# Another order for the steps of the S5 mixer in a two-layer hybrid encoder trunk

## The chip, the cores and the metric

The kernel runs on one core of a Trainium2 chip. The metric is the device time of one execution in microseconds (us). Five engines work side by side, each through its own queue of instructions and in the order of that queue: TensorE (PE, matmuls and transposes), VectorE (DVE), ScalarE (ACT), GpSimd (POOL) and SyncE (SP, here only an issuer of DMAs). ScalarE issues DMAs too, from the same queue that holds its arithmetic.

## The reference

The sequence has 1024 rows of 1024 channels. Layer 0 mixes the rows with a diagonal complex state-space layer (S5), layer 1 with gated linear attention; each is followed by a squared-ReLU MLP. The change touches the S5 mixer alone:

```python
def s5_mixer(u, a_re, a_im, log_dt, b_re, b_im, c_re, c_im, d_skip, w_glu):
    # 64 groups of 16 channels, each with a 64-dim complex diagonal state
    ...
    _, _, xr, xi = lax.associative_scan(combine, (la_re, la_im, bu_re, bu_im), axis=1)
    y = (jnp.einsum('blgp,ghp->blgh', xr, c_re.astype(f32))
         - jnp.einsum('blgp,ghp->blgh', xi, c_im.astype(f32))
         + d_skip.astype(f32).reshape(S5_GROUPS, S5_GROUP) * uf)
    z = jax.nn.gelu(y.reshape(bsz, seq, D_MODEL)).astype(u.dtype)
    val, gate = jnp.split(z @ w_glu, 2, axis=-1)
    return val * jax.nn.sigmoid(gate)
```

## The kernel before

The 1024 rows are cut into 128 chunks of 8. Within a chunk the mixer is a small Toeplitz matrix applied to the inputs; between chunks a state is carried by a scan over the 128 chunks. The channels go in 8 blocks (0 to 7) of 128 channels, and each block passes through the same kinds of step. Each step is a Python generator, and each of its pieces emits a few instructions; a piece ends at a `yield`. In what follows `s5.3` is the third piece of step `s` of block 5.

- `g` (4 groups only, for two blocks each): the adaLN shift and scale of the mixer's input. g.1 64 matmuls, g.2 and g.6 ACT copies, g.3 and g.5 PE, g.4 small DVE operations.
- `u`: u.1 scales the block's inputs on ACT (8 instructions), u.2 transposes them on PE, u.3 copies them out on ACT (8 instructions).
- `l`: the input matrices. l.1 and l.2 are two DVE products each, l.3 is 32 PE transposes into both banks of the PSUM tag `tp`, l.4 two ACT copies that free these banks.
- `p`: the rotation's sines. p.1 and p.2 DVE, p.3 ACT (Sin, Abs, Sin).
- `e`: the output matrices. e.1 and e.2 two DVE products each, e.3 and e.4 one DVE subtraction each.
- `k`: the Toeplitz block. k.1 PE matmuls into both `tp` banks, k.2 two ACT copies out of them, k.3 a short DVE addition, k.4 two DMAs from ScalarE's queue that write it to a scratch in HBM (`kd<-Ks`), k.5 one DMA from ScalarE's queue that reads it back in overlapping rows (`Tb<-kd`, 512 KB). k.5 waits in ScalarE's queue until what k.4 wrote has landed.
- `s`: the states. s.1 ACT, s.2 PE, s.3 four DVE products, s.4 two DVE additions, s.5 two DVE scans, s.6 four DVE products that give X.
- `o`: the output. o.1 PE matmuls with the Toeplitz block `Tb`, o.2 64 PE matmuls with X, o.3 two ACT Gelus.

Gelu and Sin lie in different activation tables, so ScalarE loads a table (ACT_TABLE_LOAD) wherever o.3 and p.3 take turns.

The order of all these pieces is written out by hand, in the string `S5ORD` (line 739); a loop steps the generators in that order, and a manual schedule keeps each of PE, DVE, ACT and POOL in the order of the string. SP is not in it: its loads start as buffers come free. After s7.6, VectorE splits the weights of the GLU (`wl`), and after z7 (o7.3) the last of them; the fourth weight load waits for a staging buffer. The tile pool `wa`, which holds the split weights, lies where the mixer's small tiles lay (`sp`, with `Ks` among them), so ScalarE's first splits wait for k7.4's write. Then the GLU runs, a long row of matmuls, and after it MLP 0, layer 1 and MLP 1.

The buffers around the change: `tp` 2 PSUM banks, `mm` 6, `tmp` 8, E 4, LBT 3, U 3, Tb 3, `stg` 3, and X, R8 and Ks two each.

Of the kernel before, what the change touches and what calls it, by code (L numbers as in the profile page):

```python
# [43 lines left out]
def trunk_kernel(ctx, tc, x, c, w_ada, b_ada, norm_mix, norm_mlp, s5_a_re, s5_a_im, s5_log_dt, s5_b_re, s5_b_im,  # L44
# [68 lines left out]
    def row(src, tag="row", bufs=3, pool="ww"):  # L113
        t = pools[pool].tile([P, 1024], F32, tag=tag, name="row", bufs=bufs)
        nc.sync.dma_start(out=t, in_=src.to_broadcast([P, 1024]))
        return t
# [195 lines left out]
    def small(shape, dt=F32):  # L312
        n_s[0] += 1
        return sp.tile(shape, dt, name=f"s{n_s[0]}")
# [47 lines left out]
    s1 = small(sh1)  # L362
# [23 lines left out]
    s2 = small(sh1)  # L386
# [349 lines left out]
            wg += [(h[:, 512 * k:512 * k + 512], l[:, 512 * k:512 * k + 512]) for k in range(2)]  # L736
        return wg

    S5ORD = "[ s0 s1 S7 S6 I0 S2 S3 e0 I0 S5 H1:v S0 S4 S1 e0 T0 H0:v T0 g0 l0 u0:am p0:v e0 l0 g0 g0 u0 e0 g0 u1:am p0 g0 e1 g1 g0 p0 p1:v e1 l0 g1 u0 p1 e1 e2 p1 e1 l1 l0 g2 e2 l1 g1 s0 g2 g1 e2 g1 s0 g2 u1 g1 u2:am g3 g2 u1 s0 k0 e2 s0 k0 g3 g2 g3 g2 k0 g3 k0 s2 s0 l1 p2:v e3 k0 l1 l2 g3 p2 s1 g3 l2 p2 k1 s1 u2 k1 o0 u2 k1 s1 l2 k1 u3:am s1 o0 e3 l2 s1 k1 s3 k2 e3 o0 l3 s2 k2 e3 k2 k3 l3 k2 o1 s2 k3 l3 p3:v k2 s2 p3 o1 l3 e4 p3 s2 u3 e4 o1 k3 u3 o2 e4 s2 k3 u4:am s3 e4 l4 o2 s4 s3 k3 l4 k4 o2 u4 p4:v s3 k4 u4 l4 p4 e5 p4 s3 l4 u5:am e5 o3 k4 e5 k4 s4 s5 s3 u5 e5 u6:am o3 l5 s4 k4 u5 k5 l5 o3 p5:v k5 s4 l5 p5 e6 p5 s4 l5 e6 o4 s6 k5 e6 k5 s5 s4 u6 e6 u7:am o4 l6 s5 k5 u6 k6 l6 o4 p6:v k6 s5 l6 p6 e7 p6 s5 l6 e7 o5 s7 k6 e7 k6 s6 s5 u7 e7 o5 k6 l7 u7 s6 k7 o5 l7 k7 p7:v l7 s6 p7 s6 p7 l7 k7 o6 s6 k7 s7 o6 s7 k7 s7 o6 s7 o7 s7 o7 o7 ]"

    kinds = {"u": feed, "l": tab_lb, "e": tab_e, "k": tab_k, "p": rotation, "s": states, "o": output, "g": group, "I": inputs}
    gen = {}
# [1 line left out]
    last = {}  # L744
    for n, w in enumerate(S5ORD.split()):
        if w[1:] != "7":
            continue
        last[w[0]] = n
    for n, w in enumerate(S5ORD.split()):
        if w == "[":  # L750
# [154 lines left out]
    for j in range(4):  # L905
# [29 lines left out]
        if j == 2:  # L935
            g2 = row(modr[0][4])
# [515 lines left out]
    g2 = row(modr[1][4])  # L1452
# [83 lines left out]
```

## Time and profile before

| what | value |
| --- | --- |
| time, median of 3 runs | 2200.97 us (2200.49 to 2201.13) |
| the profiled execution: its own time | 2202.5 us |
| the profiled execution: span | 2200.8 us |
| PE / DVE / ACT / POOL busy, share of the span | 96% / 66% / 32% / 18% |
| TensorE's granted clock, mean | 0.986 |
| the mixer (up to z7) | the first 187.0 us of the span |

Views are of one profiled execution and count from the start of its span. A chain of waits names, step by step, what the end waited for. In a timeline an instruction that found its engine idle has that idle time and its releaser in brackets. ACTq and SPq are the queues' DMA issues.

### The profile page before, as it was taken

The numbers are of one execution on the slowest core, as the hardware profiler recorded it, in microseconds if no ns is written. First come the engines' busy times: TensorE is split into PE (matmuls) and PEld (weight loads), VectorE is DVE, ScalarE is ACT, GpSimd is POOL, SyncE is SP. The second block draws the span as 40 slices with busy tenths as digits, with TensorE's granted clock in tenths as the row PEclk, the third lists the DMA queues.
The fourth block names the chain that finished last, engine by engine and source line by source line (L and its number), as shares of the span: only waits on it lengthen the run. The fifth ranks groups of instructions, "written<-read, shape, count | busy, mean of one in ns | idle before, by whom it ended". The sixth has DMA issues, their size and how long they took to land.

```text
span 2200.8 us, 26747 instructions
## 1 busy us (share of the span) xinstructions
PE 2117.0 (96%) x10857; PEld 1730.6 (79%) x10857; DVE 1448.7 (66%) x2004; ACT 693.9 (32%) x1163; POOL 397.1 (18%) x294
## 2 busy tenths in 40 slices
PE   5988999899999999999899999999999999999998
PEld 4876777778888888888687877787788888888886
DVE  8885767966656656656832266638866665665666
ACT  6673113422222222222521443314322222222223
POOL 0000001222222222222600000001122222222223
PEclk9989999999999999999899999999999999999999
DMA  8224771111112111111353103520111111111112
GB/s 250 58 71 138 233 245 51 49 48 57 48 48 58 48 48 58 49 48 58 129 172 99 49 30 112 170 89 29 48 48 48 58 48 48 58 48 48 58 48 105
DMA packets 107656, 176.58 MB, mean 80 GB/s; under 512 B 10463, under 2 KB 76103, under 8 KB 107469
## 3 DMA queue, kind: packets, MB, share of 16 engines
q1 hardware_dynamic: 97164, 168.71, 24.3%
q10 hardware_dynamic: 10368, 6.16, 1.3%
q8 instruction: 85, 1.39, 0.3%
q14 instruction: 39, 0.31, 0.0%
HBM read 164.45 MB, written 10.40 MB: 79 GB/s over the span
## 4 chain that ended last, share of the span: by engine, by line
PE 86%; DVE 6%; DMA 4%; ACT 2%; issue 1%; POOL 1%; ACTq 0%; SPq 0%; POOLq 0%; DVEq 0%
PE mm L216 27%; PE mm L215 27%; PE mm L217 27%; DVE tmp L56 1%; DMA Tb<-kd 1%; DMA stg<-in_w_ada_dram 1%; PE mm L1362 1%; PE tp L210 1%; DMA kd<-Ks 1%; PE tp L609 1%; PE mm L1342 1%; DVE nk L59 1%; DVE adacc L59 0%; DMA stg<-in_gla_w_out_dram 0%; DVE hT L56 0%
## 5 line engine op out<-in xcount | busy, mean ns | idle before, releaser
L56 DVE TENSOR_TENSOR big<-mm,big 128x512 f32<-128x512 f32 x528 | 343.0, 683 | 91.4 <-PE mm L217 85.5
L216 PE MATMUL mm<-w,a 128*128 128x512 f32 x1024 | 387.8, 392 | 0.9 <-DVE w L56 0.9
L217 PE MATMUL mm<-w,a 128*128 128x512 f32 x1024 | 385.4, 390 | 0.0
L215 PE MATMUL mm<-w,a 128*128 128x512 f32 x1024 | 364.8, 390 | 4.3 <-ACT w L66 4.1
L216 PE MATMUL mm<-l,rg 128*128 128x512 f32 x904 | 355.2, 393 | 5.0 <-DVE l L56 5.0
L217 PE MATMUL mm<-h,rg 128*128 128x512 f32 x904 | 354.1, 392 | 0.5 <-DVE rg L56 0.5
L215 PE MATMUL mm<-h,rg 128*128 128x512 f32 x904 | 350.2, 393 | 2.4 <-ACT h L66 1.8
L56 DVE TENSOR_TENSOR wk<-mm,wk 128x512 f32<-128x512 f32 (+1 forms) x100 | 68.8, 688 | 379.2 <-PE mm L217 320.7
L56 POOL TENSOR_TENSOR wk<-wk 128x512 f32<-128x512 f32 (+1 forms) x122 | 160.3, 1324 | 745.6 <-DMA mod<-wk 317.0
L215 PE MATMUL mm<-wh,hT 128*128 128x512 f32 (+1 forms) x768 | 290.4, 380 | 1.7 <-ACT hT L66 1.1
L217 PE MATMUL mm<-wh,hT 128*128 128x512 f32 (+1 forms) x768 | 289.7, 378 | 0.0
L216 PE MATMUL mm<-wl,hT 128*128 128x512 f32 (+1 forms) x768 | 288.9, 377 | 0.1
L56 POOL TENSOR_TENSOR wk<-wk,row 128x1024 f32<-128x1024 f32 x64 | 163.2, 2551 | 608.4 <-DMA wk<-in_w_ff_dram 399.4
L216 PEld LDWEIGHTS mm<-w,a 128*128 128x128 f32 x1024 | 192.7, 188 | 47.5 <-DVE w L56 8.3
L215 PEld LDWEIGHTS mm<-w,a 128*128 128x128 f32 x1024 | 191.2, 188 | 46.5 <-ACT w L66 5.5
L217 PEld LDWEIGHTS mm<-w,a 128*128 128x128 f32 x1024 | 192.8, 188 | 39.4
L66 ACT ACTIVATE wk<-mm 128x512 f32<-128x512 f32 x140 | 83.5, 598 | 423.5 <-PE mm L217 416.4
L216 PEld LDWEIGHTS mm<-l,rg 128*128 128x128 f32 x904 | 169.9, 188 | 43.4 <-DVE l L56 5.9
L215 PEld LDWEIGHTS mm<-h,rg 128*128 128x128 f32 x904 | 169.8, 188 | 41.4 <-ACT h L66 2.3
L217 PEld LDWEIGHTS mm<-h,rg 128*128 128x128 f32 x904 | 170.0, 188 | 39.0 <-DVE rg L56 0.8
L66 ACT ACTIVATE rg<-wk 128x1024 fp32r<-128x1024 f32 (+1 forms) x126 | 114.2, 951 | 271.7 <-POOL wk L56 270.2
L215 PEld LDWEIGHTS mm<-wh,hT 128*128 128x128 f32 x768 | 144.4, 188 | 39.3 <-issue 3.9
(244 smaller groups left out, 2628.4 us busy)
## 6 DMA issues: line engine op xcount, KB each, us to landing
wk<-in_w_ff_dram SPq DMA_DIRECT2D x128, 512.0 KB
stg<-in_w_ada_dram SPq DMA_DIRECT2D x80, 512.0 KB
stg<-in_gla_w_in_dram SPq DMA_DIRECT2D x17, 512.0 KB
stg<-in_s_w_glu_dram SPq DMA_DIRECT2D x32, 256.0 KB
row<-mod SPq DMA_DIRECT2D x10, 512.0 KB
wada<-in_w_ada_dram SPq DMA_DIRECT2D x9, 512.0 KB
big<-in_x_dram SPq DMA_DIRECT2D x8, 512.0 KB
Tb<-kd ACTq DMA_DIRECT2D x8, 512.0 KB
```

What stands on the lines that cost most here:

```text
L56: (e or V).tensor_tensor(out=out, in0=a, in1=b, op=op)
L59: V.scalar_tensor_tensor(out=out, in0=a, scalar=s, in1=b, op0=op0, op1=op1)
L66: S.activation(out=out, in_=a, func=f, **kw)
L210: ins = T.transpose(pt[:, P * k:P * k + P], h[:, P * (4 * q + k):P * (4 * q + k + 1)], ident)
L215: T.matmul(pst, ah, bh, start=first, stop=False, **kw)
L216: T.matmul(pst, ah, bl, start=False, stop=False, **kw)
L217: return T.matmul(pst, al, bh, start=False, stop=last, **kw)
L609: T.matmul(pts[i][:, P * q:P * q + P], t[i][k][:, P * q:P * q + P], (nident if i < k else ident), start=q == 0 and k == 0, stop=q == 3 and ...
L1342: T.matmul(kvp[c2][hp2][:, 256 * (h % 2):256 * (h % 2) + 256], kz[t % 2][cr, P * h:P * h + P], vo[cr, t, 256 * h:256 * h + 256], start=Tru ...
L1362: T.matmul(op[h // 2][64 * c2:64 * c2 + 64, 256 * (h % 2):256 * (h % 2) + 256], qT[:, h, n0:n0 + 64], Sc[c2][:, h, :], start=True, stop=True)
```

## The change

One string is replaced by another. Both hold the same 264 entries, each kind and block with the same number of pieces and on the same engines; the first 24 (up to e0.3) are the same. No instruction, size or buffer differs.

```diff
-    S5ORD = "[ s0 s1 S7 S6 I0 S2 S3 e0 I0 S5 H1:v S0 S4 S1 e0 T0 H0:v T0 g0 l0 u0:am p0:v e0 l0 g0 g0 u0 e0 g0 u1:am p0 g0 e1 g1 g0 p0 p1:v e1 l0 g1 u0 p1 e1 e2 p1 e1 l1 l0 g2 e2 l1 g1 s0 g2 g1 e2 g1 s0 g2 u1 g1 u2:am g3 g2 u1 s0 k0 e2 s0 k0 g3 g2 g3 g2 k0 g3 k0 s2 s0 l1 p2:v e3 k0 l1 l2 g3 p2 s1 g3 l2 p2 k1 s1 u2 k1 o0 u2 k1 s1 l2 k1 u3:am s1 o0 e3 l2 s1 k1 s3 k2 e3 o0 l3 s2 k2 e3 k2 k3 l3 k2 o1 s2 k3 l3 p3:v k2 s2 p3 o1 l3 e4 p3 s2 u3 e4 o1 k3 u3 o2 e4 s2 k3 u4:am s3 e4 l4 o2 s4 s3 k3 l4 k4 o2 u4 p4:v s3 k4 u4 l4 p4 e5 p4 s3 l4 u5:am e5 o3 k4 e5 k4 s4 s5 s3 u5 e5 u6:am o3 l5 s4 k4 u5 k5 l5 o3 p5:v k5 s4 l5 p5 e6 p5 s4 l5 e6 o4 s6 k5 e6 k5 s5 s4 u6 e6 u7:am o4 l6 s5 k5 u6 k6 l6 o4 p6:v k6 s5 l6 p6 e7 p6 s5 l6 e7 o5 s7 k6 e7 k6 s6 s5 u7 e7 o5 k6 l7 u7 s6 k7 o5 l7 k7 p7:v l7 s6 p7 s6 p7 l7 k7 o6 s6 k7 s7 o6 s7 k7 s7 o6 s7 o7 s7 o7 o7 ]"
+    S5ORD = "[ s0 s1 S7 S6 I0 S2 S3 e0 I0 S5 H1:v S0 S4 S1 e0 T0 H0:v T0 g0 l0 u0:am p0:v e0 e1 g0 g0 e0 u0 g0 u1:am e1 g0 l0 g1 g0 e1 u0 p0 k0 e1 e2 k0 p1:v g1 l0 p0 k0 e2 p1 e2 k0 p1 g2 l1 e2 l0 l1 g2 g1 e3 g2 s0 g1 g2 g1 g3 s0 g1 k0 g2 u1 g2 g3 e3 k1 u2:am e3 s0 k1 u1 l1 k1 s0 k1 p2:v s2 o0 s0 l1 g3 s1 g3 l2 g3 o0 s1 g3 k1 l2 k2 o0 e3 u2 p2 s1 k2 p2 l2 k2 s1 e4 k2 u2 o1 s1 l2 l3 o1 u3:am e4 l3 k2 s3 p3:v k3 e4 o1 s2 p3 e4 u3 e5 k3 p3 l3 s2 u3 k3 s2 l4 k3 l3 s2 u4:am k4 s3 e5 k4 s2 o2 s4 u4 l4 k3 o2 u5:am s3 u4 e5 l4 p4:v k4 e5 o2 p4 s3 k4 l4 e6 p4 k5 s3 s4 l5 o3 k5 s5 s3 u5 k4 u6:am e6 o3 l5 u5 s4 l5 o3 e6 p5:v k5 e6 k5 p5 l5 s4 p5 k6 e7 s5 s4 u6 k6 u7:am o4 l6 s4 k5 s6 u6 e7 o4 l6 s5 l6 o4 e7 p6:v k6 p6 k6 l6 e7 s5 p6 k7 s6 l7 s5 u7 k7 u7 o5 l7 s5 l7 k6 s7 s6 o5 l7 p7:v k7 p7 k7 s6 p7 s7 s6 o5 s7 o6 k7 s6 s7 o6 s7 s7 o6 o7 o7 o7 ]"
```

In words: the Toeplitz blocks' pieces come earlier in most of the blocks, with more work of other steps between k.4, k.5 and o.1, and the output matrices e of the early blocks come earlier. VectorE's work in the string between k.4 and k.5, and between k.5 and o.1, is for blocks 0 to 7 in microseconds (pieces taken at e.1 1.2, e.2 1.2, e.3 0.6, e.4 0.6, l.1 1.2, l.2 1.2, p.1 0.6, p.2 1.06, s.3 2.4, s.4 1.2, s.5 2.25, s.6 2.4, k.3 0.1, g.4 0.5):

| | 0 | 1 | 2 | 3 | 4 | 5 | 6 | 7 |
| --- | --- | --- | --- | --- | --- | --- | --- | --- |
| k.4 to k.5, before | 4.2 | 5.9 | 3.0 | 4.2 | 6.6 | 6.6 | 3.0 | 2.4 |
| k.4 to k.5, after | 7.6 | 7.1 | 6.0 | 7.1 | 7.1 | 9.3 | 8.9 | 5.9 |
| k.5 to o.1, before | 5.9 | 3.7 | 7.0 | 8.7 | 8.7 | 8.7 | 10.0 | 3.5 |
| k.5 to o.1, after | 6.0 | 7.6 | 14.8 | 11.2 | 12.4 | 12.4 | 10.0 | 8.3 |

The turns between o.3 and p.3, each with a table load, are 11 in either string.

## Rows read from the trace of the kernel before

**Rows 1.** Windows: busy us of each engine, TensorE's granted clock, DMA share, GB/s

```profile
33.19:159.70 126.51, 106.48 (x1460) 97.80 (x1459) 117.16 (x201) 86.71 (x205) 0.00 (x0) 0.93 0.32 83
159.70:176.00 16.30, 11.83 (x138) 11.01 (x136) 8.36 (x14) 6.68 (x9) 0.00 (x0) 0.92 0.41 109
176.00:187.00 11.00, 8.68 (x83) 8.10 (x83) 5.40 (x5) 1.56 (x4) 0.00 (x0) 0.69 0.51 161
```

**Rows 2.** A window of the same view in the GLU

```profile
220.00:275.00 55.00, 55.00 (x245) 43.03 (x245) 43.47 (x64) 10.48 (x18) 0.00 (x0) 1.00 0.72 233
```

**Rows 3.** Waits of VectorE, 33 to 176 us: total us, times, longest us

```profile
DVE tmp L56 <- PE mm L658: 10.5, 5, 7.9
DVE Ks L56 <- ACT Ks L66: 5.6, 2, 4.5
DVE s L56 <- PE tp L527: 0.6, 1, 0.6
```

**Rows 4.** The chain of waits at the mixer's end: start us, us, what

```profile
164.01 6.33 DMA kd<-Ks
170.43 7.18 DMA Tb<-kd
177.66 3.78 PE mm L696 x16
181.43 4.42 PE mm L704 x64
...
186.38 0.59 ACT z L711
```

**Rows 5.** Timeline of ScalarE: start us, us, what, [idle before]

```profile
127.56 0.52 ACTq L640 DMA_DIRECT2D kd<-Ks  x1
...
132.04 0.62 ACTq L644 DMA_DIRECT2D Tb<-kd  x1
...
144.35 0.53 ACTq L640 DMA_DIRECT2D kd<-Ks  x1
150.80 0.61 ACTq L644 DMA_DIRECT2D Tb<-kd  x1
151.46 2.90 ACT L66 ACTIVATE U<-mm,s 128x128 f32<-128x128 f32 x8 [6.62 <-DMA kd<-Ks]
```

**Rows 6.** Timeline of VectorE

```profile
32.59 0.68 DVE L56 TENSOR_TENSOR E<-tmp 128x512 f32<-128x512 f32 x1
...
113.50 1.29 DVE L56 TENSOR_TENSOR stg<-BB,s 128x512 f32<-128x512 f32 x2
...
129.51 1.29 DVE L56 TENSOR_TENSOR stg<-BB,s 128x512 f32<-128x512 f32 x2
...
175.28 0.68 DVE L686 TENSOR_TENSOR X<-tmp,rot 128x508 f32<-128x508 f32 x1
```

**Rows 7.** Timeline of TensorE

```profile
68.73 2.54 PE L696 MATMUL mm<-Tb,U 128*128 128x128 f32 x16 [2.24 <-DMA Tb<-kd]
...
124.99 1.95 PE L609 MATMUL tp<-ident,stg 128*128 128x128 f32 x16
126.78 1.95 PE L696 MATMUL mm<-Tb,U 128*128 128x128 f32 x16
128.66 1.97 PE L658 MATMUL mm<-U,LBT 128*64 128x128 f32 x32
130.55 1.09 PE L558 MATMUL mm<-ident,wk 128*128 128x128 f32 x8
131.58 3.84 PE L704 MATMUL mm<-E,X 64*128 64x128 f32 x64
135.35 0.69 PE L628 MATMUL tp<-E,BB 64*32 64x128 f32 x32
```

**Rows 8.** Timeline of SP's DMA issues

```profile
143.72 1.60 SPq L98 DMA_DIRECT2D stg<-in_s_w_glu_dram  x2
...
160.80 17.52 SPq L98 DMA_DIRECT2D stg<-in_s_w_glu_dram  x6
```

## The prediction

> **What bounds the kernel now.** I read the page first. TensorE is busy 96% of the span (the table above), so most of the kernel can't be moved by an order of steps; the question is where it is not the bound. Windows say where: before 187 us. From 33 to 160 us VectorE is busy 117.16 of 126.51 us and TensorE 106.48; from 160 to 176 us VectorE falls to 8.36 of 16.30, and from 176 to 187 us nobody is full [rows 1]. Later, in the GLU, TensorE is busy 55.00 of 55.00 us [rows 2]: what the mixer ends sooner, the rest starts sooner, and nothing there gives it back as long as the GLU's first weights are there.
>
> Then VectorE's waits in the mixer. There are only a few, 10.5 + 5.6 + 0.6 = 16.7 us in all, and two make up most of it: 7.9 us ahead of s7.3 for s7.2's matmuls (`mm L658`), and 4.5 us ahead of k2.3 for k2.2's copies [rows 3]. Who is behind the 7.9 us is to be followed on ScalarE. At 144.35 us it issues the last write of k6.4, it reaches k6.5 soon after, and stands there until 150.80; the copies of u7.3, next in its queue, start at 151.46 after 6.62 us idle [rows 5], and k7.2's copies come behind those. Until they have run, both `tp` banks are taken, so l7.3 waits, then l7.4, s7.2 and s7.3. The 4.5 us has in part the same source: o0.1 has waited 2.24 us in TensorE's queue for block 0's `Tb` [rows 7], and l2.3, o0.2 and k2.1 stand behind it. So both large waits start at a DMA of the Toeplitz blocks that came too late for what was queued behind it.
>
> The chain of waits shows a third loss, at the end: k7.4's write from 164.01 to 170.43, `Tb` 7.18 us to 177.66, then o7.1 3.78, o7.2 4.42 and the Gelu, z7 at 186.97 [rows 4]. X, which o.2 needs, was there at 175.28 + 0.68 = 175.96 [rows 6]. So the end waited for the DMA and not for VectorE: z7 came 11.0 us behind X.
>
> **The change part by part.** It removes and adds no instruction. VectorE's work from e0.3's end (32.59 + 0.68, about 33.2) to s7.6's end (175.96) is 142.8 us less 16.7 of waits = 126.1 us in either order [rows 3, 6]. The period of a block is 129.51 − 113.50 = 16.0 us, without a wait in it [rows 6]. So the mixer's end is 33.2 + 126.1 + VectorE's new waits + the tail from X7 to z7. Both unknowns I get by laying the new order out by hand: each engine's queue in the new sequence, with the durations of the rows, a piece starting when its engine is free and its inputs and its buffer are there.
>
> *Steady part, k.4 to k.5.* A write takes 132.04 − 127.56 = 4.5 us from its last issue, and 150.80 − 144.35 = 6.4 us or 170.43 − 164.01 = 6.4 us where SP is loading GLU weights (issues at 143.72 and from 160.80) [rows 4, 5, 8]. I take 6.4 throughout. The change puts 5.9 to 9.3 us of VectorE's work between k.4 and k.5 where there were 2.4 to 6.6. Block 3 as an example: VectorE ends k3.3 at 87.6 us, the two issues end at 88.6, the write lands at 95.0; ScalarE, after k4.2 and s4.1, comes to k3.5 at 93.9 and stands 1.1 us; `Tb` lands at 102.8, and TensorE, after l4.3, k5.1 and s4.2, comes to o3.1 at 107.0. These 1.1 us are the longest stand that I find, with some tenths at k4.5 and k5.5; behind it wait u5.1 or u6.1, whose inputs come long ahead of their use. So the 6.62 us of k6.5 goes. *k.5 to o.1*: the read takes 7.2 us [rows 4], and the new order has 6.0 to 14.8 us of VectorE's work there, and block 0's read is issued at 51.9 and lands at 59 us, ahead of TensorE's reaching o0.1 at 60.8. So o0.1's wait goes, and with it the 4.5 us: laid out, k2.2 ends at 70.6 us and VectorE comes to k2.3 at 71.5.
>
> *What takes their place.* Block 0's Toeplitz kernel now takes both `tp` banks ahead of l0.3, which starts at 41.0, only after k0.2. l0.4 then stands behind p1.3 until 47.5, s0.2 ends at 51.1, and s0.3 waits 0.9 us. Then k1.3 waits 0.7 for k1.2, g3.4 0.45 for g3.3, s1.3 0.2. (VectorE's pieces add up as in the table of the section on the change; e.g. from 33.2: e1.1, e0.4, g0.4, e1.2, l0.2, e1.3, p0.2, e1.4, e2.1, p1.1, k0.3 to 42.1, and e2.2 to g2.4 to 50.2.) From s1.6 (77.4 us) on I find none: s.2 ends 1.3 to 7 us ahead of s.3, but s7.2 only 0.2 us ahead of s7.3, behind o5.2 on TensorE. Sum 2.3 us. A lay-out by hand leaves out the lag between engines and every small surprise; before, too, the four smaller waits for s.2 make 10.5 − 7.9 = 2.6 us [rows 3]. Bounds: none more than found, 2.3; or a further 3 of about 1 us each, 5.3. I take 3.7, between them. s7.6 then ends at 33.2 + 126.1 + 3.7 = 163.0 us, 13.0 us sooner.
>
> *The tail.* k7.4 is issued right after k7.3, 15.2 us ahead of X7 (p7.2, s6.4, s6.5, s7.3, s6.6, s7.4, s7.5 and s7.6 follow on VectorE: 1.06 + 1.2 + 2.25 + 2.4 + 2.4 + 1.2 + 2.25 + 2.4); its two issues take 1 us, its write, at 6.4, lands 7.8 us before X7, and `Tb`, 7.2 later, some 0.7 us before X7. So o7.1 mostly overlaps with s7.6's end instead of following a late DMA. What is left is o7.1 and o7.2 and z7. At the full clock o.1 is 1.95 and o.2 3.84 [rows 7], the tail 1.25 + 3.84 + 1.1 = 6.2; at the clock of the old end (0.69 granted from 176 to 187 us [rows 1], o7.1 3.78, which is 1.95 at the lower of its two levels, 1.2 GHz, and o7.2 4.42, mostly at the upper [rows 4]) it is 3.1 + 4.42 + 1.1 = 8.6. TensorE again waits ahead of o7.1, though about 1 us and not 6; I take the middle, 7.4, so 3.6 us sooner than 11.0.
>
> *DMAs beside others.* The row says that a write next to SP's loads takes 6.4 us instead of 4.5 [rows 5, 8]. The Trainium skill ("DMA: Bandwidth & Descriptors", Issuing engines are not separate DMA queues) says that DMAs started by any engine run on the same 16 DMA engines and interleave; the trace agrees (6.4 against 4.5 us). It speaks against a gain at the last block, where the GLU's loads come as well; the rival for it is below.
>
> *The GLU's weights.* They need a staging buffer (l7.3 done), the pool `wa` (k7.4's write landed) and VectorE after s7.6. In my lay-out l7.3 ends 17 us sooner and k7.4's write as well, so all move along. The fourth load waits for the first split on VectorE, right behind s7.6; it has the tail's 7.4 us and not 11.0 to land. One window without that cover would cost 1 to 2 us; I leave it at nothing, since the split of the fourth waits for z7 in ScalarE's queue anyhow. Table loads: 11 turns in both, nothing. POOL's queue has no moved step; SP's only follow buffers.
>
> **The sum.** 13.0 + 3.6 = 16.6 us off the profiled execution's own 2202.5 gives 2185.9; the median of the runs lies 1.5 below it, so 2184.3 us.
>
> **The rivals.**
> - *TensorE's loop becomes the bound.* In the new order l.3 of a block is followed by k.1 of the next, which needs the `tp` banks that l.4 still holds; nothing lies between to cover. Its round is l.3 3.8 (half of it 1.95), k.1 0.7, s.2 2.0, u.2 1.1, o.1 1.95 and o.2 3.84 [rows 7], 13.4 us, and about 1.2 for l.4's copies: 14.6 us at full clock, 13.4/0.93 + 1.2 = 15.6 at the granted 0.93 [rows 1], against VectorE's 16.0. If each of seven rounds slips 1 us past VectorE, 7 us are lost: 2191. It turns the result to slower when a round takes 16 + 21/7 = 19 us or more, that is when the granted clock averages under 13.4/17.8 = 0.75; then the time is over 2205, and at a mean of 0.7 (20.3 us a round, 30 us lost) it is 2214. For it: the clock did fall to 0.69 where TensorE idled [rows 1]. Against: it idles less in the new order, and s.2 starts with some us in hand.
> - *The last block's DMAs collide with the weights.* If the read of `Tb` is slowed as the write was (6.4/4.5), it takes 10.2 us instead of 7.2: 3 us more tail, 2187 to 2188. For it: the loads lie there. Against: before, the read of block 7 ran beside issues until 178 [rows 8] and still took 7.18 [rows 4].
> - *The order doesn't do what it says.* The old waits go, but l.4, s.2 or u.3 come late in each block instead, and VectorE's waits sum to 13 to 17 us again; only the tail's 3.6 is won or less: 2197 to 2201. My lay-out speaks against it.
>
> **How the numbers follow.** The forecast, with its own range of 2180 to 2188 (the bounds of waits and tail: 2.3 and 6.2 give 2181.7, 5.3 and 8.6 give 2187.1, a little added): 0.64. DMA collision, 2187 to 2190: 0.08. TensorE's loop by 1 us or so a round, 2189 to 2195: 0.15. No gain by the third rival: 0.06. Slower, by the loop or otherwise: 0.07. At most 16.7 + 11.0 − 6.2 = 21.5 us can be won, so 2179 is the floor; the range is 2179 to 2194 and leaves out the last two and the far end of the third. About 0.2% (4.4 us) is what a measurement of this kernel can tell from no change: faster 0.87, same 0.06, slower 0.07.
>
> **What would show it.** Right: VectorE's waits from 33 us to s7.6 sum to 2 to 6 us, none over 2; ScalarE idles under 2 us at any k.5; s7.6 ends at 161 to 165 us, z7 at 168 to 172; the GLU's windows look as before. Wrong: waits of a microsecond or more in every block ahead of s.3 with TensorE as releaser (the loop); `Tb` landing some us behind X7; TensorE waiting for weights at the GLU's start.

## The result, and the profile after

The changed kernel takes 2190.22 us (median, 2188.20 to 2191.83) where the kernel before takes 2201.05 beside it: 0.9949 of the time, 95% interval 0.9932 to 0.9966. That is 10.8 us sooner, inside the stated range of 2179 to 2194, but outside the forecast's own 2180 to 2188, and 5.9 us short of the 2184.3 forecast. The profiled execution took 2189.98 us, with a span of 2188.3.

What the order did to the mixer is read first, in VectorE's waits from 33 us to s7.6's end, the rows that answer to [rows 3] (total us, times, longest us):

```profile
DVE tmp L56 <- ACT rot L66: 4.2, 1, 4.2
DVE tmp L56 <- PE mm L658: 1.3, 1, 1.3
DVE Ks L56 <- ACT Ks L66: 0.9, 1, 0.9
DVE s L56 <- PE tp L527: 0.2, 1, 0.2
```

The 16.7 us of before are 6.6 now. Both large waits are gone, and the three small ones that the lay-out found are there: s0.3 1.3 us (laid out 0.9), k1.3 0.9 (0.7), g3.4 0.2 (0.45). The 4.2 us (4.25 in the timeline, ahead of s7.3) were not foreseen. Windows of all engines say where they lie; the first row answers to [rows 1], the last to [rows 2] (busy us of each engine, TensorE's granted clock, DMA share, GB/s):

```profile
33.19:150.00 116.81, 107.27 (x1509) 98.52 (x1509) 113.68 (x196) 86.45 (x205) 0.00 (x0) 0.96 0.39 98
150.00:160.00 10.00, 4.30 (x38) 3.67 (x36) 5.75 (x9) 4.98 (x6) 0.00 (x0) 0.76 0.35 74
...
170.00:180.00 10.00, 3.30 (x12) 2.13 (x11) 5.34 (x6) 3.40 (x6) 0.00 (x0) 0.62 0.69 218
220.00:275.00 55.00, 55.00 (x241) 43.03 (x240) 42.61 (x64) 9.86 (x17) 0.00 (x0) 1.00 0.70 228
```

Up to 150 us VectorE is full; the GLU's long stretch is full on TensorE, as before. Two holes stand between, at 150 to 160 and at 170 to 180 us. For the first, ScalarE's timeline (start us, us, what, [idle before]):

```profile
146.48 1.18 ACTq L640 DMA_DIRECT2D kd<-Ks  x2
147.70 1.15 ACT L66 ACTIVATE rot<-tmp 128x512 f32<-128x512 f32 x2 [2.36 <-DVE tmp L59]
148.76 1.04 ACT L66 ACTIVATE wh<-stg 128x1024 fp32r<-128x1024 f32 x1
153.53 1.06 ACT L66 ACTIVATE wh<-stg 128x1024 fp32r<-128x1024 f32 x1 [3.73 <-DMA kd<-Ks]
153.76 0.62 ACTq L644 DMA_DIRECT2D Tb<-kd  x1
154.50 0.70 ACT L66 ACTIVATE rot<-rot,k_pi 128x512 f32<-128x512 f32 x1
```

The reader is to see the `wh` lines between the first two and the last of p7.3's three activations. These are the GLU's first weight splits. They are not in `S5ORD`, and two of them came to stand here in ScalarE's queue, in front of the last sine. The second stands 3.73 us for k7.4's write (whose source `Ks` lies under its target in `wa`). The sine comes out at 155.20 us, and s7.3, which needs it, starts at 155.23, 4.25 us late. s7.6 ends at 165.94 where 163.0 was laid out.

The second hole is seen in the chain of waits behind s7.6:

```profile
165.93 3.42 DVE wl L56 x3
169.37 5.94 DMA stg<-in_w_ada_dram
175.51 1.11 issue
176.62 1.22 DVE wl L56
...
178.59 1.09 PE tp L789 x4
```

z7 isn't on it. Before, the chain ran from the Toeplitz write and read through o7.1, o7.2 and z7 [rows 4] on to these:

```profile
186.97 0.95 ACT wh L66
187.95 1.23 DVE wl L56
...
189.83 1.11 PE tp L789 x4
```

Now it runs from VectorE's part of the first three splits into a load of adaLN weights that SP can issue only when the splits have freed the staging buffers, and then through VectorE's queue, as its timeline shows:

```profile
165.25 0.69 DVE L686 TENSOR_TENSOR X<-tmp,rot 128x508 f32<-128x508 f32 x1
165.84 3.50 DVE L56 TENSOR_TENSOR wl<-stg,wh 128x1024 fp32r<-128x1024 f32 x3
174.24 0.75 DVE L63 TENSOR_SCALAR adacc<-stg,csil 128x1024 f32<-128x1024 f32 x1 [4.90 <-DMA stg<-in_w_ada_dram]
175.42 1.28 DVE L59 SCALAR_TENSOR_TENSOR adacc<-stg,csil,adacc 128x1024 f32<-128x1024 f32 x1 [0.42 <-DMA stg<-in_w_ada_dram]
176.62 1.22 DVE L56 TENSOR_TENSOR wl<-stg,wh 128x1024 fp32r<-128x1024 f32 x1
```

TensorE's timeline beside it:

```profile
178.59 1.09 PE L789 MATMUL tp<-ident,z 128*128 128x128 f32 x4 [4.12 <-DVE hT L56]
```

z7 ends at 171.18, 15.8 us sooner than before, 5.2 us behind X7's end instead of 11.0. But the fourth split's difference `wl` stands behind the first two operations of the adaLN sum (`adacc`) in VectorE's queue, and they wait 4.90 us for their weights. TensorE stands 4.12 us for what comes behind `wl`, and the GLU's products run on from 178.59 instead of 189.83: 11.2 us sooner, and that is what the time shows. So 4.6 of the 15.8 us were lost between z7 and the GLU. In VectorE's timeline of before the same place reads:

```profile
185.72 1.29 DVE L59 SCALAR_TENSOR_TENSOR adacc<-stg,csil,adacc 128x1024 f32<-128x1024 f32 x1 [0.43 <-DMA stg<-in_w_ada_dram]
187.95 1.23 DVE L56 TENSOR_TENSOR wl<-stg,wh 128x1024 fp32r<-128x1024 f32 x1 [0.94 <-ACT wh L66]
```

There VectorE was through with the sum's first operations at 187.01 and waited 0.94 us for the fourth split, which waits for z7.

### The profile page after: what moved, and what is told of

Read it like the earlier page. It is cut to its first block, busy times and chain, and to the rows that moved or that the text cites. A ratio compares the mean times of both kernels' runs of the same rounds, so it can differ in the third digit from the quotient of the medians.

```text
span 2188.3 us, 26758 instructions
## 1 busy us (share of the span) xinstructions
PE 2112.1 (97%) x10857; PEld 1726.8 (79%) x10857; DVE 1447.4 (66%) x2004; ACT 692.9 (32%) x1163; POOL 397.0 (18%) x294
## 3 DMA queue, kind: packets, MB, share of 16 engines
q8 instruction: 85, 1.39, 0.3%
## 4 chain that ended last, share of the span: by engine, by line
PE 88%; DVE 6%; DMA 3%; ACT 2%; issue 1%; POOL 0%; SPq 0%; ACTq 0%; POOLq 0%; DVEq 0%
PE mm L216 27%; PE mm L215 27%; PE mm L217 27%; DMA stg<-in_w_ada_dram 1%; DVE tmp L56 1%; PE tp L609 1%; PE mm L1362 1%; PE tp L210 1%; PE mm L1342 1%; PE mm L704 1%; DMA stg<-in_s_w_glu_dram 0%; PE mm L658 0%; DVE adacc L59 0%; DMA stg<-in_gla_w_out_dram 0%; DVE nk L59 0%
## 5 line engine op out<-in xcount | busy, mean ns | idle before, releaser
L216 PEld LDWEIGHTS mm<-l,rg 128*128 128x128 f32 x904 | 170.6, 189 | 43.1 <-DVE l L56 5.6
L215 PEld LDWEIGHTS mm<-h,rg 128*128 128x128 f32 x904 | 170.2, 188 | 41.5 <-ACT h L66 2.3
```

Source lines behind the costliest of these rows:

```text
L215: T.matmul(pst, ah, bh, start=first, stop=False, **kw)
L216: T.matmul(pst, ah, bl, start=False, stop=False, **kw)
```

## The experiments

In what follows, *tail* is z7's end less X7's end. The medians of before in the three sets of runs were 2201.32, 2201.51 and 2202.28 us, and 2200.20 beside the last kernel.

**The splits, and the sum.** Two edits, alone and together, and both in the old order. The first keeps the three splits behind z5 in ScalarE's queue, the second keeps the adaLN sum behind the fourth split's difference in VectorE's:

```diff
-    with tc.issue_after(lastx[-1].ins):
+    with tc.issue_after(lastx[-1].ins), tc.issue_after(lastz[5].ins):
         wg = glu_weights(0, range(3))
```

> The new order, with ScalarE's splits of the first three GLU weights held back until o5.3's Gelu (they stood between p7.3's sines). Theory A (these splits, which wait for k7.4's write, make s7.3 late, and s7.6 sets the GLU's start through the loads and VectorE's sums behind it): VectorE's wait of 4.25 us ahead of s7.3 is gone, s7.6 ends near 162 us instead of 165.9, the GLU starts some 4 us sooner, 2186 to 2187 us. Theory B (the end is set by the last Toeplitz block's DMA, whatever VectorE does): z7 and the GLU's start stay, 2190 us.

2185.86 us, 0.9924 of before (0.9911 to 0.9938): 4.4 us sooner than the change by the medians (runs of 2184.27 to 2186.60 against 2188.20 to 2191.83). In VectorE's timeline s7.3 starts without a wait at 150.85, and the queue behind it reads:

```profile
169.56 0.75 DVE L63 TENSOR_SCALAR adacc<-stg,csil 128x1024 f32<-128x1024 f32 x1 [4.62 <-DMA stg<-in_w_ada_dram]
...
171.94 1.22 DVE L56 TENSOR_TENSOR wl<-stg,wh 128x1024 fp32r<-128x1024 f32 x1
```

X7 ends at 161.53, 4.4 us sooner, and all the rest with it: VectorE's end alone carries the time. The tail is 8.0 us here, longer than the change's 5.2, and that cost nothing.

```diff
         wg += glu_weights(0, (3,))
+    w4 = lastw[0].ins        # the instruction of the fourth difference
...
+                with tc.issue_after(w4) if (j, t) == (0, 1) else nullcontext():
                     acc = ada_sum(*ADA[0])
```

> The new order, with VectorE's first adaLN sum held behind the split of the fourth GLU weight (before, it stood ahead of it and waited 4.90 us for its load). Theory A: the fourth split follows z7's split on ScalarE at once, near 174 us instead of 176.6 to 177.8, the first full row of matmuls starts near 174.5 instead of 178.6, 2186 to 2187 us. Theory B (the loads behind it come later by the same amount and the GLU gives it back further on): 2189 to 2190 us.

2190.53 us (2186.82 to 2192.86), 0.9946 (0.9933 to 0.9958): no gain over the change.

> Both edits of the two runs before. Theory A: they add up, since one moves s7.6 and the other shortens what follows z7: GLU's start near 171 to 172 us, 2182 to 2184 us. Theory B for both: 2189 to 2190 us. In between (one covers the other): 2186 us.

2185.96 us (2184.17 to 2189.03), 0.9927 (0.9915 to 0.9940): the first edit's gain and no more.

> The same two edits with the old order of steps. Theory A: nothing, since there the splits stand behind p7.3 already and the sums' loads land ahead of z7: 2200 to 2202 us. If the edits are worth something by themselves, whatever the order: 2194 to 2197 us.

2202.66 us (2199.83 to 2204.91), 1.0001 (0.9992 to 1.0010). So neither edit is worth anything without the new order: what they take away is a cost that the new order brought up.

That the sum's place does act is seen where the path behind the mixer is measured from both of its starts, first in eight profiles (us; *ada row* is the start of the first product of the adaLN rows, the `L191` group, some 30 us into the GLU):

| | X7 ends | z7 ends | ada row | from X7 | from z7 |
| --- | --- | --- | --- | --- | --- |
| before | 175.96 | 186.97 | 217.2 | 41.2 | 30.2 |
| the change | 165.94 | 171.18 | 206.3 | 40.4 | 35.1 |
| splits behind z5 | 161.53 | 169.48 | 202.0 | 40.5 | 32.5 |
| reads behind writes (below) | 190.86 | 196.40 | 232.2 | 41.3 | 35.8 |
| one read later (below) | 172.23 | 177.73 | 213.3 | 41.1 | 35.6 |
| sum moved | 169.68 | 175.38 | 207.4 | 37.7 | 32.0 |
| both | 164.38 | 173.82 | 205.9 | 41.5 | 32.1 |
| both, old order | 173.00 | 183.93 | 216.1 | 43.1 | 32.2 |

Above the sum's move the distance from X7 is the constant one (40.4 to 41.3, with tails of 5.2 to 11.0 us); with the sum moved it is the distance from z7 (32.0 to 32.2). The change made z7 early and left the path from X7 as long as it was. In the two profiles of the new order with the sum moved, the gain was lost further ahead: their TensorE had fallen to its lower clock at 137 us (below). The profiles of the six kernels that follow widen both distances and keep the pattern: with the sum in its old place 39.2 to 41.8 us from X7 (29.7 to 35.8 from z7) over all such profiles, with the sum moved 30.8 to 32.3 us from z7 (37.7 to 43.1 from X7). So the sum's place shifts the path, but in the medians no gain from it was measured.

**The distance between write and read.** Each k.5 put back right behind its k.4, all else in the new order; for the last two blocks:

```diff
- ... k6 p6 k6 l6 e7 ... s5 l7 k6 s7 s6 ... k7 p7 k7 s6 p7 s7 s6 o5 s7 o6 k7 s6 s7 ...
+ ... k6 p6 k6 k6 l6 e7 ... s5 l7 s7 s6 ... k7 p7 k7 k7 s6 p7 s7 s6 o5 s7 o6 s6 s7 ...
```

> The changed order with one thing undone: each block's k.5 (the read that spreads Tb) stands right behind its k.4 (the write of kd) in ScalarE's queue, as in most blocks of the old order; all else stays where the change put it, the tables far ahead too. Theory A (the gain is the distance between k.4 and k.5, filled with ScalarE's other work): ScalarE stands 4 to 6 us behind each write, its sines and evacuations come that much later, VectorE waits for ScalarE again by 8 us or more in the stretch from 33 us to s7.6, and the time is 2198 to 2205. Rival B (the gain comes from the tables e and l standing far ahead, the distance matters little): ScalarE's stands are seen, VectorE waits under 8 us, and the time is 2190 to 2194. By the prediction's own terms (4.9 us a block off ScalarE, 8 blocks, of which VectorE feels only what outlasts its own work) I hold A.

2219.01 us, 1.0085 (1.0071 to 1.0099), 28.8 us over the change and 17.5 over before. ScalarE stands at the reads, as in this line of its timeline, and VectorE's waits from 33 us to s7.6 show what it costs:

```profile
138.53 1.08 ACT L66 ACTIVATE LBT<-tp 128x512 f32<-128x512 f32 x2 [4.57 <-DMA kd<-Ks]
```

```profile
DVE tmp L56 <- PE mm L658: 13.3, 6, 4.2
DVE tmp L56 <- ACT rot L66: 12.2, 2, 11.1
DVE s L56 <- PE tp L527: 5.1, 2, 3.1
```

30.6 us of waits instead of 6.6, and X7 24.9 us later. The price was under-expected by 14 us at least; most of that is at the last block, whose sines now stand behind k7.5, 7.1 us on ScalarE and, in the second row, 11.1 on VectorE. So the new order can't do without this distance. But this kernel has the reads nearer than the old order had them (there 2.4 to 6.6 us of VectorE's work lay between, and at block 7 the sines stood ahead of k7.5), and it is 17.5 us slower than before. How much of the 10.8 us comes from the distance, and how much from the tables e and l standing further ahead, no run here parts.

**One read later in the old order.** The reverse: one stall of before taken away, alone.

```diff
- ... k7 o5 l7 k7 p7:v ...     (k6.5 ahead of l7.1 and u7.3)
+ ... k7 o5 k6 l7 k7 p7:v ...  (k6.5 behind z5)
```

> The old order with one step moved: block 6's read k6.5 behind z5, so that the copies of U (2.9 us), a table load (1.28) and z5 (1.09) fill the 6.6 us that ScalarE stood there. Theory A (the stall in ScalarE's queue is what VectorE pays for, at the next step that needs ScalarE): ScalarE comes to k7.2 and the last sines about 5 us sooner, VectorE's wait of 7.9 us ahead of s7.3 falls to 3 to 4, s7.6 ends at 171 to 172, and the time is 2196 to 2198. Rival B (that wait is TensorE's, with its clock, and not ScalarE's): the wait stays over 6 and the time is 2200 to 2202.

2199.38 us (2195.71 to 2203.14), 0.9990 (0.9981 to 0.9998): 2.9 us sooner by the medians, with an interval of 0.4 to 4.2 us, between the two expectations. X7 ended 3.7 us sooner in the profile, but some 2.5 of these were there at 122 us already, far ahead of the moved step (k2.3's wait was 1.83 us here and 4.55 before), and so aren't its doing. u7.3's copies ran at 144.51 instead of 151.46 [rows 5], so ScalarE's stall did go; VectorE's wait ahead of s7.3 did not. TensorE's timeline, and VectorE's:

```profile
157.84 2.68 PE L696 MATMUL mm<-Tb,U 128*128 128x128 f32 x16 [3.96 <-DMA Tb<-kd]
160.45 0.70 PE L658 MATMUL mm<-U,LBT 128*64 128x128 f32 x4
```

```profile
163.93 2.48 DVE L56 TENSOR_TENSOR tmp<-mm,rot 128x512 f32<-128x512 f32 x4 [8.44 <-PE mm L658]
```

o6.1 now stands 3.96 us for `Tb` in TensorE's queue, with s7.2 behind it. So theory A's stall and theory B's wait are both there: the read that is late for ScalarE's queue when it stands early is late for TensorE's when it stands late, and the write itself has to come sooner.

**The DMAs beside the writes.** From the two profiles with the sum moved I took block 6's write to be long (7.7 us up to k6.5) where SP's first GLU load was issued ahead of it. A copy of a column into the staging tile, in ScalarE's queue behind the write, holds that load back:

```diff
+    def gate(n):
+        for _ in range(n):
+            s = stg()
+            act(s[:, 0:1], ident[:, 0:1], AF.Copy)
+            early.append(s)
...
-            s = stg()
+            s = early.pop(0) if early else stg()
...
         for r in range(2):
             S.dma_start(out=kd[b]..., in_=Ks[:, r, :])      # (shortened)
+        if b == 6:           # in the second kernel behind k7.5: if b == 7: gate(3)
+            gate(1)
```

> The changed kernel with the first three GLU splits behind z5, and SyncE's first GLU load (two transfers of 256 KB) held until ScalarE has issued block 6's write of kd, by a copy of one column of the staging tile in ScalarE's queue. Theory C (the write is long, 7.7 us against under 5, where SyncE's loads were issued before it, and short where they came after it): the write of block 6 takes at most 5.1 us, k6.5 goes out by 140, and the time is that of the splits alone, 2184 to 2186.5, with no run above 2187. Rival D (the length of the write is chance, or set by something else): a length of 7 us or more though the load comes after it, or runs spread to 2189 as without the hold.

2185.03 us (2184.46 to 2186.23), 0.9930 (0.9917 to 0.9942).

> The same with all of SyncE's first three GLU loads (1.5 MB) held until ScalarE has issued block 7's read k7.5. The last two blocks' writes and reads then have the DMA engines to themselves. Theory C: the writes of blocks 6 and 7 take about 4 us, k7.5 goes out at 151 to 152 and o7.1 no longer waits for Tb; z7 is limited by VectorE's X alone, 168.5 or sooner; the time is 2183 to 2186 if the loads still land before the splits are wanted (about 163), and 2187 to 2192 if the fourth split then comes late. Rival D: writes and read as long as with the loads beside them (about 6 and 7.2 us).

2185.33 us (2184.55 to 2189.62), 0.9934 (0.9921 to 0.9946).

> The hold of the first GLU load behind block 6's write, the first three splits behind z5, and the first adaLN sum behind the fourth split. Theory C with the sum's place worth what the profiles showed behind z7 (some 3 us from z7 to the first product of the adaLN rows): block 6's write at most 5.1 us, s7.6 ends at 161 to 162, the fourth split's difference stands right behind z7, and the time is 2181.5 to 2184. Rival E (the sum's place is worth nothing, since the time behind z7 is set by another chain): 2185 to 2187, as with the splits alone.

2189.61 us, with runs at 2182.40, 2185.13, 2189.61, 2189.70 and 2190.37; 0.9946 (0.9932 to 0.9960).

The column lies in one of a load's two transfers, so one transfer was held and the other went ahead; in the second kernel six of the eight came behind k7.5. There block 7's write took at most 3.8 us (its issue ends at 146.98, k7.5 goes out at 150.76) against 5.9 beside the loads (147.58 to 153.50 with the splits alone). The Trainium skill ("DMA: Bandwidth & Descriptors", Issuing engines are not separate DMA queues) says that DMAs started by ScalarE, SyncE or GpSimd run on the same 16 DMA engines and interleave; these two numbers agree. But the time is the same, 2185.3 and 2185.9, and this kernel doesn't show what the collision costs, since the held loads then ran beside the read. k7.5 went out at 150.76, 2.7 us sooner, and yet o7.1 started at 160.64, against 160.99 with the splits alone:

```profile
160.64 3.65 PE L706 MATMUL mm<-Tb,U 128*128 128x128 f32 x16 [3.47 <-DMA Tb<-kd]
```

From k7.5's issue to o7.1's start that is 9.9 us instead of 7.5, and ScalarE stood 8.53 us for the held loads. So the collision moved from the write to the read. With the splits alone the chain of waits runs through X7 and the adaLN load, and o7.1's wait for `Tb` isn't on it; in *both* and in the three kernels of the next part it is, with 7.6 to 8.2 us of write and 7.1 to 8.0 us of read. A kernel with the sum moved and the loads held behind `Tb`'s landing was not run. Theory C fell with the third kernel, whose runs spread by 8 us although the load was held. (Its profiled run, 2182.40, is the shortest of all: with the sum moved and the full clock from 130 to 147 us, the ada row came at 199.04, against 201.43 with the load held alone.)

**TensorE's clock.** C had misread the profiles. In both, ScalarE came to k6.5 late because copies ahead of it waited for TensorE, not for the write. TensorE's timeline with the splits behind z5, then with the sum moved:

```profile
135.36 1.13 PE L628 MATMUL tp<-E,BB 64*32 64x128 f32 x32 [1.39 <-ACT LBT L66]
136.42 1.97 PE L658 MATMUL mm<-U,LBT 128*64 128x128 f32 x32
```

```profile
136.31 1.57 PE L628 MATMUL tp<-E,BB 64*32 64x128 f32 x32 [2.28 <-ACT LBT L66]
137.81 3.68 PE L658 MATMUL mm<-U,LBT 128*64 128x128 f32 x32
141.42 1.81 PE L558 MATMUL mm<-ident,wk 128*128 128x128 f32 x8
```

TensorE stands ahead of k7.1 for l6.4's copies (`LBT`), which stand behind k6.4 in ScalarE's queue, and k6.4 waits for VectorE's k6.3. VectorE was 1.0 us later in the second execution at 72 us already (its chain has the scan there at 72.85, the other at 71.85). The gap was 2.28 us instead of 1.39, about as much longer, and behind it s6.2 took 3.68 us instead of 1.97: the granted clock from 136 to 142 us is 0.51, the lower of the two levels (1.2 GHz), against 1.00 (2.4 GHz). The change itself had 1.17 and kept the clock there; *both* had 2.40 and lost it (there VectorE was 0.5 us later than with the splits alone, and TensorE 0.5 sooner). To close the gap I moved k6.4 behind the copies:

```diff
- ... p6:v k6 p6 k6 l6 e7 s5 ...
+ ... p6:v k6 p6 l6 k6 e7 s5 ...
```

> The changed order with the first three GLU splits behind z5, and one more step moved: block 6's write k6.4, which waits for VectorE's k6.3, stands behind the two copies of LBT (l6.4) in ScalarE's queue instead of ahead of them. I now read theory C wrong: in the two long profiles k6.5 stood behind copies that waited for TensorE, whose clock had fallen. Theory F: TensorE's gap ahead of k7.1 (1.2 to 1.5 us in the profiles that kept the full clock, 2.3 and 2.4 in the two that lost it for some 7 us) comes from k6.4's wait for VectorE, and decides the run. With the copies ahead of k6.4 the gap is under 0.7, the granted clock from 130 to 145 is 1.00, and all runs lie at 2184 to 2186.5. Rival G (the spread has another cause): a gap under 0.7, and yet runs above 2187.5.

2187.78 us (2184.16 to 2190.20), 0.9937 (0.9925 to 0.9949).

> The same with the first adaLN sum behind the fourth split's difference too, the kernel whose runs lay at 2182.4, 2185 and three times 2190 with the load held. Theory F: all runs at 2181.5 to 2184, none at 2187 or above, and the sum's place is worth some 3 us. Rival G: two groups of runs again, one near 2190. Rival E (the sum's place is worth nothing): one group at 2185 to 2186.

2187.72 us (2186.26 to 2192.94), 0.9942 (0.9928 to 0.9956).

A miss: the gap did not close, it got another cause, block 7's E (e7.4), which k7.1 needs too. TensorE's timeline of the one, then of the other:

```profile
136.12 0.67 PE L628 MATMUL tp<-E,BB 64*32 64x128 f32 x24 [1.75 <-DVE E L56]
136.73 1.97 PE L658 MATMUL mm<-U,LBT 128*64 128x128 f32 x32
```

```profile
136.43 1.11 PE L628 MATMUL tp<-E,BB 64*32 64x128 f32 x24 [1.75 <-DVE E L56]
137.47 3.12 PE L658 MATMUL mm<-U,LBT 128*64 128x128 f32 x32
```

The same gap, once with the full clock behind it and once without. So these two say nothing for the edit, and the gap's length alone doesn't decide. Two other places of the same profiles say so too. In all ten profiles of the new order with its reads in place TensorE stands 2.8 us ahead of k4.1, and in nine the clock falls behind it; in that of the loads held behind k7.5 it doesn't, and there it falls behind a stand of 1.50 us ahead of k6.1 (0.50 granted from 121 to 123 us). TensorE's timeline of the change, then of that kernel:

```profile
90.64 1.56 PE L628 MATMUL tp<-E,BB 64*32 64x128 f32 x32 [2.82 <-ACT LBT L66]
92.14 3.68 PE L658 MATMUL mm<-U,LBT 128*64 128x128 f32 x32
```

```profile
90.01 1.13 PE L636 MATMUL tp<-E,BB 64*32 64x128 f32 x32 [2.82 <-ACT LBT L66]
91.06 1.97 PE L668 MATMUL mm<-U,LBT 128*64 128x128 f32 x32
...
118.54 1.13 PE L636 MATMUL tp<-E,BB 64*32 64x128 f32 x32 [1.50 <-ACT LBT L66]
119.60 3.63 PE L668 MATMUL mm<-U,LBT 128*64 128x128 f32 x32
```

VectorE didn't wait at either place: what a fall of the clock costs goes by what stands behind it. The last kernel moves e7.4 too:

```diff
- ... o4 e7 p6:v k6 p6 k6 l6 e7 s5 ...
+ ... o4 e7 e7 p6:v k6 p6 l6 k6 s5 ...
```

> The kernel of the last run with one more step moved: VectorE's e7.4, which block 7's k7.1 waited for there (1.75 us in both profiles, one of which lost TensorE's full clock behind it), stands right behind e7.3, ahead of p6.1 and k6.3. Theory F (TensorE's gap ahead of k7.1 decides whether the clock falls, and that the time): the gap is under 0.7, the granted clock from 130 to 145 is 1.00, s6.2 takes 1.97 us, and all runs lie within 2 us of each other at 2181.5 to 2184.5. Rival G (the spread from 2182 to 2190 has another cause, the gap at k7.1 being one of several places): runs still over 2187 though the gap is closed in the profile. A loss is possible too: k6.3 and the last sines come 0.7 us later.

2185.59 us (2183.61 to 2186.86), 0.9927 (0.9914 to 0.9941). The gap is closed, and TensorE's timeline shows where it went:

```profile
131.84 1.40 PE L628 MATMUL tp<-E,BB 64*32 64x128 f32 x32
133.17 1.97 PE L658 MATMUL mm<-U,LBT 128*64 128x128 f32 x32
...
150.64 3.75 PE L696 MATMUL mm<-Tb,U 128*128 128x128 f32 x16 [3.42 <-DMA Tb<-kd]
```

s6.2 keeps its 1.97 us, the clock from 130 to 147 us is 1.00, and no run lies above 2187, as F says. But not at F's 2181.5 to 2184.5: TensorE, at k7.1 some 3 us sooner now, stands 3.42 us at o6.1 for `Tb`, and loses the clock there (0.50 from 150 to 155 us, o6.1 in 3.75 us).

Over the 49 runs of the ten kernels in the new order with the reads in their new places, those with a mean granted clock of 0.990 or more (17 runs) took 2182.4 to 2185.6 us, those with 0.987 or less (12 runs) 2189.0 to 2192.9. That the spread goes with the clock is shown; where the long runs of a kernel lose it is known only for the executions that were profiled, and of these, two lost it at this gap for some 6 us, one for a shorter time, and the last kernel's at another gap. So theory F is not shown, and rival G, several places, stands.

No kernel here is measurably better than the splits behind z5 alone (2185.86): the others with that edit lie from 2185.0 to 2189.6 us, none clearly apart from it on the short side. It is faster than the change and than before.

## Why the prediction was right, and where it was short

- *The time.* 2190.22 us misses the forecast's own 2180 to 2188 (0.64). It lies in the band that was given to TensorE's loop, 2189 to 2195 (0.15), and that loop didn't come. The stated range held only because it was widened for that rival, and what used it up was something else, so that much is luck: the new order brought GLU splits into ScalarE's last sines, and most of the gain in the tail could not arrive.
- *Steady part.* Right. Up to block 6 the profile shows no idle time of ScalarE at a read (the 0.50 us at 74.67 us lie behind k2.4's issues), both large waits are gone, those found by the lay-out are where it had them. At block 7 the wait for the write, 3.73 us, fell on the split that stood ahead of k7.5; with the splits moved ScalarE stood 2.23 us at k7.5, just over the 2 us that were named, and not on the chain of waits. Putting all reads right behind their writes cost 28.8 us. One thing the reading of the 7.9 us left out: TensorE had stood 4.18 us ahead of l7.3 and ran it from 157 to 161 us at a granted clock of 0.50, in 6.37 us (`156.98 6.37 PE tp L609 x32` in the chain of waits) instead of the 3.8 that the prediction has for l.3; in the new order it took 3.7. So part of that wait was the clock, behind the late DMA.
- *VectorE's waits, 3.7 us.* Measured 6.6, outside the named "2 to 6 us, none over 2". The unforeseen part is the 4.25 us ahead of s7.3. With the splits out of the way X7 ended at 161.53, 14.4 us sooner, against 13.0 forecast: without that surprise the term would have been a little too careful, and the time 2185.86, 1.5 us from the forecast.
- *The GLU's weights.* The sentence that failed first: "In my lay-out l7.3 ends 17 us sooner and k7.4's write as well, so all move along", "I leave it at nothing". The splits stand in no written order; before, they ran at 171.10 us, behind the sines, and in the new order two of them stood between the last sines. This is the step of the prediction that failed by most. The 1 to 2 us named there were for another thing, the landing of the fourth load; this cost 4.3 us on VectorE (4.4 in the time).
- *The tail, 3.6 us.* The tail itself shrank more than forecast: 5.8 us, to 5.2, less than the 6.2 that I had taken for the least. (o7.1 started ahead of X7's end, at 164.25, so only o7.2 and z7 lay behind it. That it could is due to X7's being late: with the splits moved the tail was 8.0, near the 7.4 forecast.) But the sum added it whole, and the sum is where it failed: in the trace of before VectorE, through with the first adaLN operations, waited only 0.94 us for the fourth split. So the path from X7 through the staging buffers and the adaLN load was 0.94 us shorter than the one through z7, and of any gain in the tail about that much could arrive. The fall in this stretch was 1.2 us (13.9 to 12.7 from X7 to the GLU's run).
- *The sum.* 13.0 + 3.6 = 16.6 forecast; 10.0 from VectorE + 1.2 behind it = 11.2 measured at the GLU's start, 10.8 in the medians.
- *The rivals.* TensorE's loop did not become the bound; but its clock, which that rival named for it, goes with a spread of 5 to 8 us between runs, in single gaps rather than in each round. The collision of the last block's DMAs is there for the write (5.9 against 3.8 us); the read took 7.1 to 8.0 us in the chains that hold it, and not the 10.2 that this rival feared, but 9.9 from its issue to o7.1's start where the held loads ran beside it. In the change the read is not on the chain of waits; the write is, by the split that stood for it. That the order doesn't do what it says is out: VectorE's waits sum to 6.6 us and not to 13 to 17.

## What to carry to other kernels

When a stage ends on two paths, read from the trace how far the second is behind the first before you count a gain on the first: the wait of an engine that joins them (here 0.94 us of VectorE for the split) bounds what can arrive, unless the second path gets shorter too (1.2 us did). A step that stands in no written order moves too when its inputs come sooner, and may land in front of something that has no slack; look in the new order for the free places in each queue that it could take. And a DMA's wait, moved from one in-order queue, turns up in the next (ScalarE's k.5, then TensorE's o.1) unless the transfer itself is started sooner.

## What was unexpected of the hardware

Ahead of k7.1, stands of TensorE of 2.28 and 2.40 us were followed by the lower clock (0.51 and 0.50 granted from 136 to 142 us), stands of 1.02 to 1.51 us were not, and 1.75 us was once and once not. Elsewhere in the same profiles 2.82 us was once not followed by it, and 1.50 us once was, so the length of the stand before it doesn't tell by itself. The lower clock made s6.2 3.68 us instead of 1.97 and the products with `wk` 1.81 instead of 1.09. In one of the two cases the longer stand came from a microsecond of VectorE, lost before 72 us. The same 2 x 120 KB write took at most 3.8 us with six of the eight weight transfers held back, and 8.21 us in the chain of the kernel with the write behind the copies and the sum moved; what it held up went by the queue behind it as well as by its length.
